# Squared-ReLU layers: running sums of the seven products in PSUM, sums of weight blocks by adding transfers

## The chip, the core and the metric

One Trainium2 chip, one core, one launch. The metric is device time in microseconds, the median of repeated executions of the whole program. The core's engines are named as in the profile: PE (TensorE, matrix products), ACT (ScalarE), DVE (VectorE), POOL (GpSimd) and SP (SyncE, which issues nearly all transfers). SBUF is the on-chip memory, PSUM the small memory in which matmuls add up.

## The reference

Four residual layers on an input of 512 frames by 1024 features in float32: banded attention, a squared-ReLU layer (the MLP), a Griffin recurrent block, a second MLP, each with an RMS norm ahead; at the end one more norm. The change lies in the two MLPs:

```python
def sq_relu_mlp(h, w1, w2):          # w1: 1024 x 4096, w2: 4096 x 1024
    z = jax.nn.relu(jnp.einsum('bsd,df->bsf', h, w1))
    return jnp.einsum('bsf,fd->bsd', z * z, w2)
...
        h = h + sq_relu_mlp(rmsnorm(h, norm_mlp[layer]), mlp_w1[layer], mlp_w2[layer])
```

## The kernel before

**Arithmetic.** A float32 operand is kept as two tiles, H (rounded) and L (what is left over), and each product is three matmuls, H by H, H by L and L by H (`mm3`, lines 202 to 204). So each block of weights, once it has landed, is cast by ACT (`wh`, line 132) and subtracted by DVE (`wl`, line 135) before PE can use it. A weight unit is one such pair of 128 x 1024.

**Weight units.** `plan` is a list of units in the order in which PE uses them. `fetch` issues the transfer, the cast and the subtraction of the next one; `want` hands units to PE, and keeps fetching some units ahead. Eight buffers hold `wh` and `wl` in the MLPs, so the cast of a unit waits until PE has done with the unit eight places ahead of it.

**MLP.** The hidden width of 4096 is cut in eight stretches of 512, the groups g = 0 to 7. Group 0 is computed plainly (tiles `u`). Groups 1 to 7 use a scheme with seven products in place of eight: 512 rows and 256 columns of w1 make a block, and four blocks, 11, 21, 22 and 12, make a group. Beside the blocks themselves the scheme needs four sums of them, s1 = 21 + 22, s3 = 11 + 21, s2 = s1 + 11 and s4 = s2 + 12. Before, DVE makes them in place (lines 128 and 129, tiles `b`). On the other side stand the pieces B11, B21, B22 of the normed input and four sums of them, t1 to t4, made once in a layer. A product is 24 matmuls of 128 x 256 into a PSUM tile `p`. PSUM has two pools that matter here: "at" for the products and "mm" for `d` and `u`, with four buffers each.

The seven products go into four quarters of the group's result (`cA` and `cB`, each 128 x 2 x 512, with a left half LO and a right half HI). Written with P for a product: cA LO = P1 + P2; cA HI = P1 + P6 + P5 + P3; cB HI = P1 + P6 + P7 + P5; cB LO = P1 + P6 + P7 + P4. Before, ACT copies P1 out (line 646, into `w`) and DVE adds the others from PSUM, one by one (lines 651 to 666). Then follow ReLU with the norm's factor (line 628), the square (ACT, line 619), the split into `zH` (ACT, line 622) and `zL` (DVE, line 623).

**Down units.** The second weight matrix multiplies `z` of a group into eight PSUM tiles `d`, each of 12 matmuls of 128 x 512, which DVE adds to the residual `h` (line 678). While the products of group g run, the down units of group g − 1 are placed between them: two after the second product, one after each of the next four, two after the last. So PE runs products and down units in turn, and four weight units of the down kind (`plain`) stand between the seven of a group in `plan`.

**Order.** Each engine runs its own queue in a fixed order. A scheduler sets these orders when the program is built, from the order in the code and its own estimates of when operands are ready; on the chip an instruction whose operand isn't there holds everything behind it on its engine. SP issues the loads of the blocks (line 123); each of the four block tiles `b11`, `b21`, `b22`, `b12` has one buffer, so a group's load waits for the last use of the same tile in the group before.

Names in what follows: `wh43` is the cast unit 43 of the plan; `cA00` and `cB00` are the result of layer 0, group 0; `zH001` its second half; `p201` the product P2 of layer 0, group 1; `d000` and `d001` the first two down tiles; a trailing number after an underscore is a buffer's number.

Of the kernel before, what the change touches and what calls it, by code (L numbers as in the profile page):

```python
# [15 lines left out]
P = 128  # L16
# [24 lines left out]
def trunk(ctx: ExitStack, tc: tile.TileContext, xT, cols, win, wqkv, wo, rwin, rga, rgx, rwo, w1, w2, out):  # L41
# [54 lines left out]
    raws, start_ = {}, []  # L96

    def fetch():
# [20 lines left out]
        else:  # L119
            if kind == "11":  # L120
                for name, src in zip(("11", "21", "22", "12"), srcs):
                    raws[name] = state["raw"].tile([P, 1024], F32, name=f"b{name}_{i}", tag=f"b{name}")
                    nc.sync.dma_start(raws[name].rearrange("p (k c) -> p k c", k=4), src.rearrange("(k p) c -> p k c", p=P))

            for name, at_, with_ in (("s1", "21", "22"), ("s2", "22", "11"), ("s4", "12", "22")):
                if kind == name:
                    if kind == "s1":
                        V.tensor_add(raws["11"], raws["11"], raws["21"])
                    V.tensor_add(raws[at_], raws[at_], raws[with_])
            raw = raws[{"s1": "21", "s2": "22", "s3": "11", "s4": "12"}.get(kind, kind)]  # L130
# [4 lines left out]
        low = V.tensor_sub(L[:, :n], raw[:, :n], f(H[:, :n]))  # L135
        if not i:
            start_.append(low)
# [33 lines left out]
    def add_mlp(layer):  # L171
        starts.append(len(plan))
        for g in range(9):
# [4 lines left out]
            if g < 8:  # L178
                rows, cs = (slice(0, T), slice(T, D)), (slice(g * T, g * T + U), slice(g * T + U, (g + 1) * T))
                srcs = [w1[layer][rows[k], cs[c]] for k, c in ((0, 0), (0, 1), (1, 1), (1, 0))]  # L180
                up_ = [(kind, 4, srcs) for kind in ("11", "s1", "12", "22", "s2", "s4", "s3")]
# [19 lines left out]
    def mm3(acc, WH, WL, XH, XL, start, stop):  # L201
        PE.matmul(acc, WH, XH, start=start, stop=False)  # L202
        PE.matmul(acc, WH, XL, start=False, stop=False)  # L203
        PE.matmul(acc, WL, XH, start=False, stop=stop)  # L204
# [335 lines left out]
    def constants(behind):  # L540

        ap = cst[:, C_AP : C_AP + KT]
        e, ng, zz, z2 = (per.tile([P, KT], F32, name=f"sp{i}") for i in range(4))
# [34 lines left out]
    def mlp(ly, norm, nxt, halves):  # L578
        with ExitStack() as mctx:
# [29 lines left out]
            def product(acc, xs):  # L609
                WH, WL = want(1)  # L610
                for j in range(2):
                    for k, (XH, XL) in enumerate(xs):
                        mm3(acc[:, j * U : (j + 1) * U], WH(k, PAIR[j]), WL(k, PAIR[j]), XH, XL, k == 0, k == 3)
# [19 lines left out]
            def up(g):  # L633
# [7 lines left out]

                cA = cp.tile([P, 2, T], F32, name=f"cA{ly}{g}", tag="cA")
# [3 lines left out]
                S.copy(w, acc["1"])  # L646
                yield
                one("5", t1)
                yield
                one("2", B21)  # L650
                V.tensor_add(cA[:, :, LO], acc["2"], w)
                yield
                one("4", t4)
                yield
                one("6", t2)
                V.tensor_add(w, acc["6"], w)
# [277 lines left out]
```

## Time and profile before

| | |
|---|---|
| median of 3 runs | 1082.8 us (1082.6 to 1083.53) |
| profiled execution | 1082.37 us, span 1080.6 us |
| PE busy | 1069.6 us (99%) |
| DVE busy | 863.5 us (80%) |
| ACT busy | 531.3 us (49%) |
| POOL busy | 9.0 us (1%) |
| transfers | 111.15 MB, mean 103 GB/s |
| mean granted TensorE clock | 0.998 |

The span runs from the first to the last instruction in the trace. Busy time is time in which an engine executes; waiting isn't counted. The table's shares are means over the span; the windows below show them by stage. Layer 0's MLP lies at about 250 to 585 us, layer 1's at about 735 to 1070; the seven-product groups of layer 0 begin at 268.6, those of layer 1 at 751.7.

### The profile page before, as it was taken

What the parts mean: (1) busy time and instruction counts of PE and PEld (TensorE: products, weight loads), DVE (VectorE), ACT (ScalarE), POOL (GpSimd) and SP (SyncE); (2) the same over time, 40 slices, a digit from 0 to 9 for tenths busy, and PEclk for the clock granted to TensorE, in tenths of its full rate; (3) what the DMA queues carried; (4) which work ended last, traced back from release to release, by engine and by line L of the source; (5) the groups of instructions that cost most, each with busy time, mean ns of one, the idle gap of its engine ahead of it and who ended that gap; (6) DMA issues with size and microseconds to landing.
All of it is one profiled execution on the core that took longest, in us unless ns stands there. A gap on an engine that the chain in (4) does not pass through costs nothing.

```text
span 1080.6 us, 15337 instructions
## 1 busy us (share of the span) xinstructions
PE 1069.6 (99%) x6046; PEld 935.6 (87%) x6046; DVE 863.5 (80%) x1286; ACT 531.3 (49%) x775; POOL 9.0 (1%) x28
## 2 busy tenths in 40 slices
PE   9999999999999999999999999999999999999996
PEld 7888888888899999898988888888889999989896
DVE  6889788879887787776777989879887777787665
ACT  6667567565443343342444688366443343343321
POOL 0010000000000000000000000000000000000000
PEclk9999999999999999999999999999999999999999
DMA  8354253341432323322232222442431432332102
GB/s 275 98 140 134 59 176 98 83 152 59 137 117 79 117 89 107 99 81 96 76 122 77 78 64 73 151 142 68 147 117 59 136 98 79 117 94 83 59 1 79
DMA packets 112919, 111.15 MB, mean 103 GB/s; under 512 B 4176, under 2 KB 106704, under 8 KB 112848
## 3 DMA queue, kind: packets, MB, share of 16 engines
q1 hardware_dynamic: 112560, 109.99, 33.1%
q8 instruction: 47, 0.77, 0.3%
q14 instruction: 24, 0.20, 0.1%
q10 hardware_dynamic: 288, 0.20, 0.1%
HBM read 103.87 MB, written 2.10 MB: 98 GB/s over the span
## 4 chain that ended last, share of the span: by engine, by line
PE 96%; DVE 2%; ACT 1%; DMA 1%; issue 0%; SPq 0%; DVEq 0%; ACTq 0%
PE d L203 11%; PE d L202 11%; PE d L204 11%; PE p L204 9%; PE p L203 9%; PE p L202 9%; PE x L414 1%; PE wo L203 1%; PE wo L202 1%; PE ro L202 1%; PE v L202 1%; PE ro L204 1%; PE v L204 1%; PE wo L204 1%; PE xb L202 1%; PE xb L204 1%
## 5 line engine op out<-in xcount | busy, mean ns | idle before, releaser
L132 ACT CAST wh<-wr 128x1024 fp32r<-128x1024 f32 (+1 forms) x129 | 133.6, 1039 | 201.6 <-PE d L203 88.8
L203 PE MATMUL d<-zL,wh 128*128 128x512 f32 (+1 forms) x544 | 206.3, 379 | 0.0
L202 PE MATMUL d<-zH,wh 128*128 128x512 f32 (+1 forms) x544 | 205.1, 379 | 0.0
L204 PE MATMUL d<-zH,wl 128*128 128x512 f32 (+1 forms) x544 | 204.8, 377 | 0.0
L132 ACT CAST wh<-b 128x1024 fp32r<-128x1024 f32 x98 | 101.3, 1047 | 174.8 <-PE p L203 76.0
L135 DVE TENSOR_TENSOR wl<-wr,wh 128x1024 fp32r<-128x1024 f32 (+1 forms) x130 | 156.2, 1203 | 23.3 <-ACT wh L132 23.1
L135 DVE TENSOR_TENSOR wl<-b,wh 128x1024 fp32r<-128x1024 f32 x98 | 118.7, 1219 | 42.9 <-ACT wh L132 42.8
L204 PE MATMUL p<-tH,wl 128*128 128x256 f32 x448 | 126.8, 283 | 0.0
L203 PE MATMUL p<-tL,wh 128*128 128x256 f32 x448 | 126.8, 283 | 0.0
L202 PE MATMUL p<-tH,wh 128*128 128x256 f32 x448 | 126.6, 282 | 0.0
L204 PEld LDWEIGHTS d<-zH,wl 128*128 128x128 f32 x544 | 102.4, 188 | 19.1
L202 PEld LDWEIGHTS d<-zH,wh 128*128 128x128 f32 x544 | 102.5, 189 | 16.8
L203 PEld LDWEIGHTS d<-zL,wh 128*128 128x128 f32 x544 | 102.7, 189 | 16.3 <-DVE zL L623 0.5
L678 DVE TENSOR_TENSOR h<-d,h 128x512 f32<-128x512 f32 x120 | 82.2, 686 | 38.9 <-PE d L204 38.3
L204 PE MATMUL p<-hnH,wl 128*128 128x256 f32 x336 | 95.1, 283 | 0.0
L203 PE MATMUL p<-hnL,wh 128*128 128x256 f32 x336 | 95.1, 283 | 0.0
L202 PE MATMUL p<-hnH,wh 128*128 128x256 f32 x336 | 94.9, 282 | 0.0
L202 PEld LDWEIGHTS p<-tH,wh 128*128 128x128 f32 x448 | 85.8, 192 | 1.6
L203 PEld LDWEIGHTS p<-tL,wh 128*128 128x128 f32 x448 | 85.8, 192 | 1.6
L204 PEld LDWEIGHTS p<-tH,wl 128*128 128x128 f32 x448 | 85.8, 192 | 0.0
L202 PEld LDWEIGHTS p<-hnH,wh 128*128 128x128 f32 x336 | 64.3, 191 | 1.7
L203 PEld LDWEIGHTS p<-hnL,wh 128*128 128x128 f32 x336 | 64.3, 191 | 1.6
(336 smaller groups left out, 2071.6 us busy)
## 6 DMA issues: line engine op xcount, KB each, us to landing
wr<-in_w SPq DMA_DIRECT2D x72, 512.0 KB, 3.5
b<-in_w SPq DMA_DIRECT2D x56, 512.0 KB, 4.4
wr<-in_wqkv SPq DMA_DIRECT2D x20, 512.0 KB, 4.0
wr<-in_rwin SPq DMA_DIRECT2D x16, 512.0 KB, 3.6
wr<-in_wo SPq DMA_DIRECT2D x8, 512.0 KB, 4.2
wr<-in_rwo SPq DMA_DIRECT2D x8, 512.0 KB, 3.4
x<-in_xT SPq DMA_DIRECT2D x8, 256.0 KB, 4.3
bias<-in_win SPq DMA_DIRECT2D x4, 512.0 KB, 4.5
```

The lines of the kernel that those rows point to most:

```text
L132: S.copy(H[:, :n], raw[:, :n])
L135: low = V.tensor_sub(L[:, :n], raw[:, :n], f(H[:, :n]))
L202: PE.matmul(acc, WH, XH, start=start, stop=False)
L203: PE.matmul(acc, WH, XL, start=False, stop=False)
L204: PE.matmul(acc, WL, XH, start=False, stop=stop)
L414: PE.transpose(b[:, c : c + P], pt[:, seg[t] + kt * P : seg[t] + (kt + 1) * P], ident)
L678: V.tensor_add(hT[m], acc, hT[m])
```

## The change

**Sums of weight blocks.** The four additions of DVE in a group go. In their place POOL issues four transfers a group that read a block from DRAM and add it onto a tile in SBUF (`accum_op=ALU.add`). Block 22 is added onto tile 21 right behind the loads: s1. Block 21 is added onto tile 11, once 11 itself has been cast and subtracted: s3. Block 11 is added onto tile 21, once s1 has been cast and subtracted: s2. Block 12 is added onto tile 21, once s2 has been: s4. The order of the units in `plan` and of the loads changes accordingly.

**Running sums in PSUM.** A group uses three product tiles in place of seven. P6, P7 and P4 run on in the tile of P1, and P3 runs on in that of P5. Between them ACT copies the intermediate sums out: P1 to cA LO, P1 + P6 to cA HI, the last sum to cB LO, and P5 to `w`. DVE adds three times from PSUM in place of seven. The next product on a tile waits for the copy or addition that reads it. The order of the products becomes P1, P5, P2, P6, P7, P3, P4.

**Small things.** The small tiles of `constants` lie in a work tile, and the scratch memory for transfers that POOL issues is doubled.

```diff
@@ -93,7 +93,7 @@
 
     plan = []
     state = {"next": 0, "ready": [], "ahead": 4, "stop": None, "more": None, "units": 0}
-    raws, start_ = {}, []
+    raws, srcs_, start_ = {}, {}, []
 
     def fetch():
         i = state["next"]
@@ -117,22 +117,25 @@
                 queue.dma_start(rv[:, :, c0 : c0 + w], src.rearrange("(k p) c -> p k c", p=P))
                 c0 += w
         else:
+
+            def view(name):
+                return raws[name].rearrange("p (k c) -> p k c", k=4)
+
             if kind == "11":
-                for name, src in zip(("11", "21", "22", "12"), srcs):
+                srcs_.update(zip(("11", "21", "22", "12"), (src.rearrange("(k p) c -> p k c", p=P) for src in srcs)))
+                for name in ("11", "21", "12", "22"):
                     raws[name] = state["raw"].tile([P, 1024], F32, name=f"b{name}_{i}", tag=f"b{name}")
-                    nc.sync.dma_start(raws[name].rearrange("p (k c) -> p k c", k=4), src.rearrange("(k p) c -> p k c", p=P))
-
-            for name, at_, with_ in (("s1", "21", "22"), ("s2", "22", "11"), ("s4", "12", "22")):
-                if kind == name:
-                    if kind == "s1":
-                        V.tensor_add(raws["11"], raws["11"], raws["21"])
-                    V.tensor_add(raws[at_], raws[at_], raws[with_])
-            raw = raws[{"s1": "21", "s2": "22", "s3": "11", "s4": "12"}.get(kind, kind)]
+                    nc.sync.dma_start(view(name), srcs_[name])
+                G.dma_start(view("21"), srcs_["22"], accum_op=ALU.add)
+            raw = raws[{"s1": "21", "s2": "21", "s3": "11", "s4": "21"}.get(kind, kind)]
         if i:
             S.copy(H[:, :n], raw[:, :n])
         else:
             start_.append(V.tensor_copy(H[:, :n], raw[:, :n]))
         low = V.tensor_sub(L[:, :n], raw[:, :n], f(H[:, :n]))
+        for done, name, src in (("11", "11", "21"), ("s1", "21", "11"), ("s2", "21", "12")):
+            if kind == done:
+                G.dma_start(view(name), srcs_[src], accum_op=ALU.add)
         if not i:
             start_.append(low)
         state["ready"].append((nk, H[:, :n].rearrange("p (k c) -> p k c", k=nk), L[:, :n].rearrange("p (k c) -> p k c", k=nk)))
@@ -178,7 +181,7 @@
             if g < 8:
                 rows, cs = (slice(0, T), slice(T, D)), (slice(g * T, g * T + U), slice(g * T + U, (g + 1) * T))
                 srcs = [w1[layer][rows[k], cs[c]] for k, c in ((0, 0), (0, 1), (1, 1), (1, 0))]
-                up_ = [(kind, 4, srcs) for kind in ("11", "s1", "12", "22", "s2", "s4", "s3")]
+                up_ = [(kind, 4, srcs) for kind in ("11", "s1", "12", "s2", "s3", "s4", "22")]
             else:
                 up_ = []
             dn = [("plain", 4, [w2[layer][(g - 1) * T : g * T, u * U : (u + 1) * U]]) for u in range(4)]
@@ -198,10 +201,10 @@
     add_mlp(1)
     state["stop"] = starts[0] + 4
 
-    def mm3(acc, WH, WL, XH, XL, start, stop):
-        PE.matmul(acc, WH, XH, start=start, stop=False)
-        PE.matmul(acc, WH, XL, start=False, stop=False)
-        PE.matmul(acc, WL, XH, start=False, stop=stop)
+    def mm3(acc, WH, WL, XH, XL, start, stop, shared=False):
+        PE.matmul(acc, WH, XH, start=start, stop=False, skip_group_check=shared)
+        PE.matmul(acc, WH, XL, start=False, stop=False, skip_group_check=shared)
+        PE.matmul(acc, WL, XH, start=False, stop=stop, skip_group_check=shared)
 
     def project(accs, cols_, WH, WL, xs, mid=None):
 
@@ -540,7 +543,8 @@
     def constants(behind):
 
         ap = cst[:, C_AP : C_AP + KT]
-        e, ng, zz, z2 = (per.tile([P, KT], F32, name=f"sp{i}") for i in range(4))
+        room = wk.tile([P, T], F32, name="room", tag="nsq", bufs=2)
+        e, ng, zz, z2 = (room[:, i * KT : (i + 1) * KT] for i in range(4))
         after(V.tensor_scalar(ng, ap, -1.0, None, ALU.mult), behind)
         V.tensor_tensor(e, ap, ng, ALU.max)
         S.activation(e, e, AF.Exp, scale=-1.0)
@@ -606,11 +610,14 @@
             sum_ = lambda n: [(tH[k][:, n], tL[k][:, n]) for k in range(4)]
             B11, B21, B22 = own(0, LO), own(4, LO), own(4, HI)
 
-            def product(acc, xs):
+
+
+            def product(acc, xs, fresh=True):
                 WH, WL = want(1)
                 for j in range(2):
                     for k, (XH, XL) in enumerate(xs):
-                        mm3(acc[:, j * U : (j + 1) * U], WH(k, PAIR[j]), WL(k, PAIR[j]), XH, XL, k == 0, k == 3)
+                        c = acc[:, j * U : (j + 1) * U]
+                        mm3(c, WH(k, PAIR[j]), WL(k, PAIR[j]), XH, XL, fresh and j == 0 and k == 0, k == 3, True)
 
             def pair(acc):
                 return acc.rearrange("p (j c) -> p j c", j=2)
@@ -639,31 +646,33 @@
                     product(acc[n], xs)
                     acc[n] = pair(acc[n])
 
+                def more(n, xs):
+                    product(acc[n].rearrange("p j c -> p (j c)"), xs, False)
+
                 cA = cp.tile([P, 2, T], F32, name=f"cA{ly}{g}", tag="cA")
                 cB = cp.tile([P, 2, T], F32, name=f"cB{ly}{g}", tag="cB")
                 w = pair(wk.tile([P, T], F32, name=f"w{ly}{g}", tag="nsq", bufs=2))
                 one("1", B11)
-                S.copy(w, acc["1"])
+                S.copy(cA[:, :, LO], acc["1"])
                 yield
                 one("5", t1)
+                S.copy(w, acc["5"])
                 yield
                 one("2", B21)
-                V.tensor_add(cA[:, :, LO], acc["2"], w)
+                V.tensor_add(cA[:, :, LO], acc["2"], cA[:, :, LO])
                 yield
-                one("4", t4)
+                more("1", t2)
+                S.copy(cA[:, :, HI], acc["1"])
                 yield
-                one("6", t2)
-                V.tensor_add(w, acc["6"], w)
-                V.tensor_add(cA[:, :, HI], acc["5"], w)
+                more("1", t3)
+                V.tensor_add(cB[:, :, HI], acc["1"], w)
                 yield
-                one("3", B22)
-                V.tensor_add(cA[:, :, HI], acc["3"], cA[:, :, HI])
+                more("5", B22)
+                V.tensor_add(cA[:, :, HI], acc["5"], cA[:, :, HI])
                 relu2(g, 0, cA, ALU.max)
                 yield
-                one("7", t3)
-                V.tensor_add(w, acc["7"], w)
-                V.tensor_add(cB[:, :, LO], acc["4"], w)
-                V.tensor_add(cB[:, :, HI], acc["5"], w)
+                more("1", t4)
+                S.copy(cB[:, :, LO], acc["1"])
                 relu2(g, 1, cB, ALU.min)
                 yield
 
@@ -920,7 +929,7 @@
         "rwin": a["rec_w_in"][0], "rga": a["rec_w_ga"][0], "rgx": a["rec_w_gx"][0], "rwo": a["rec_w_o"][0],
         "w1": a["mlp_w1"], "w2": a["mlp_w2"],
     }
-    nc = _bacc.Bacc("TRN2", target_bir_lowering=False, num_devices=1, dynamic_dma_scratch_size=1024)
+    nc = _bacc.Bacc("TRN2", target_bir_lowering=False, num_devices=1, dynamic_dma_scratch_size=2048)
     arrays, args = {}, []
     for name, v in arrs.items():
         v = np.ascontiguousarray(v)
```

What this does to the engines' queues at the places that matter, as the two programs stand (not how long anything takes). First ACT in the first group of layer 0's MLP, before:

```order
L132 CAST wh41_2682<-b12_38_2666 128x1024
L132 CAST wh42_2741<-wr42_2743 128x1024
L646 COPY w01_2817<-p101_2818 128x512
L619 ACTIVATE cA00_2656<-cA00_2656 128x1024
L622 CAST zH000_2780<-cA00_2656 128x1024
L619 ACTIVATE cB00_2657<-cB00_2657 128x1024
L132 CAST wh44_2819<-b22_38_2664 128x1024
L622 CAST zH001_2811<-cB00_2657 128x1024
L132 CAST wh45_2850<-wr45_2852 128x1024
```

and after:

```order
L132 CAST wh43_2748<-b21_38_2662 128x1024
L132 CAST wh44_2821<-b11_38_2660 128x1024
L132 CAST wh45_2851<-wr45_2853 128x1024
L132 CAST wh41_2683<-b12_38_2664 128x1024
L132 CAST wh42_2742<-wr42_2744 128x1024
L626 ACTIVATE cA00_2656<-cA00_2656 128x1024
L629 CAST zH000_2782<-cA00_2656 128x1024
L132 CAST wh46_2882<-b21_38_2662 128x1024
L626 ACTIVATE cB00_2657<-cB00_2657 128x1024
L656 COPY cA01_2817<-p101_2820 128x2x256
L629 CAST zH001_2813<-cB00_2657 128x1024
L659 COPY w01_2819<-p501_2850 128x512
```

The casts of s2 (`wh43`), s3 (`wh44`) and the next down unit (`wh45`) moved ahead of the two casts that stood first; s4 (`wh46`) stands between the split of `cA00` and the square of `cB00`. Both `wh43` and `wh46` read tile 21, and so an adding transfer.

PE in the same group, behind P5 (the second product in its order), before:

```order
L202 MATMUL d000_2885<-zH000_2780,wh40_2676 128x512
L202 MATMUL d001_2899<-zH000_2780,wh40_2676 128x512
L202 MATMUL p201_2913<-hnH4_80,wh41_2682 128x256
L203 MATMUL p201_2913<-hnL4_88,wh41_2682 128x256
L204 MATMUL p201_2913<-hnH4_80,wl41_2683 128x256
L202 MATMUL p201_2913<-hnH5_81,wh41_2682 128x256
L203 MATMUL p201_2913<-hnL5_89,wh41_2682 128x256
L203 MATMUL d000_2885<-zL000_2781,wh40_2676 128x512
```

and after (the fourth row shown is the first to use `zH001`, the eighth the first to use `zL001`; three rows that read like the first three are left out):

```order
L205 MATMUL d000_2886<-zH000_2782,wh40_2677 128x512
L206 MATMUL d000_2886<-zL000_2783,wh40_2677 128x512
L207 MATMUL d000_2886<-zH000_2782,wl40_2678 128x512
...
L205 MATMUL d000_2886<-zH001_2813,wh40_2677 128x512
L205 MATMUL d001_2900<-zH000_2782,wh40_2677 128x512
L206 MATMUL d001_2900<-zL000_2783,wh40_2677 128x512
L207 MATMUL d001_2900<-zH000_2782,wl40_2678 128x512
L206 MATMUL d000_2886<-zL001_2814,wh40_2677 128x512
L207 MATMUL d000_2886<-zH001_2813,wl40_2678 128x512
```

Before, matmuls of `p201` are mixed into the two down tiles; after, the 24 matmuls of `d000` and `d001` stand together and `p201` follows them.

POOL issues four transfers in each group, such as the first four here: s1, s3, s2, s4 (the fifth begins the next group).

```order
L129 DMA b21_82_4108<-in_w1 128x4x256
L138 DMA b11_82_4106<-in_w1 128x4x256
L138 DMA b21_82_4108<-in_w1 128x4x256
L138 DMA b21_82_4108<-in_w1 128x4x256
L129 DMA b21_93_4477<-in_w1 128x4x256
```

ACT in the same stretch, after, where unit 83 is s1:

```order
L132 CAST wh83_4157<-b21_82_4108 128x1024
L665 COPY cA04_3957<-p104_3960 128x2x256
L132 CAST wh84_4187<-wr84_4189 128x1024
L132 CAST wh85_4207<-b12_82_4110 128x1024
L132 CAST wh86_4256<-wr86_4258 128x1024
```

Before, POOL had no instruction in the MLPs, and no copy from PSUM stood between these casts.

## The prediction

> **What bounds the kernel now.** I read the engines and the chain of waits on the page first, then the busy time by stretch, the costliest groups, the DMA issues, and last the timelines where a layer begins.
>
> ```profile
> PE 1069.6 (99%) x6046; PEld 935.6 (87%) x6046; DVE 863.5 (80%) x1286; ACT 531.3 (49%) x775; POOL 9.0 (1%) x28
> ...
> PE 96%; DVE 2%; ACT 1%; DMA 1%; issue 0%; SPq 0%; DVEq 0%; ACTq 0%
> ```
>
> ```profile
> 0.00:130.00 130.00, 128.25 (x647) 107.92 (x648) 107.24 (x251) 88.15 (x191) 7.16 (x23) 1.00 0.52 147
> 130.00:250.00 120.00, 118.98 (x593) 99.16 (x592) 100.98 (x214) 75.04 (x154) 1.87 (x5) 1.00 0.39 119
> 250.00:1000.00 750.00, 749.88 (x4317) 661.49 (x4316) 603.82 (x738) 345.01 (x397) 0.00 (x0) 1.00 0.32 99
> 1000.00:1080.60 80.60, 72.46 (x495) 67.05 (x493) 51.45 (x85) 23.12 (x35) 0.00 (x0) 0.97 0.14 46
> ```
>
> The second fence has one stretch a row: its length, then the busy time of PE, PEld, DVE, ACT and POOL. TensorE (PE) is the bound and it isn't a mean that hides a stage: in the 750 us that hold both MLPs but the end of the second, it stands for 0.12 us. All it lacks in the whole span is 1.75 + 1.02 + 0.12 + 8.14 = 11.0 us, 1% of it, and most of that lies in the final norm, which the change doesn't touch. So the change can't gain by relieving VectorE (DVE) or ScalarE (ACT) as such. What matters is whether it makes PE stand.
>
> **What is removed from the vector engines.**
>
> ```profile
> L129 DVE TENSOR_TENSOR b<-b,b 128x1024 f32<-128x1024 f32 x42 | 51.1, 1216 | 0.0
> L128 DVE TENSOR_TENSOR b<-b,b 128x1024 f32<-128x1024 f32 x14 | 17.1, 1224 | 0.4
> L660 DVE TENSOR_TENSOR cA<-p,cA 128x512 f32<-128x512 f32 x14 | 9.7, 691 | 27.0 <-PE p L204 27.0
> L646 ACT COPY w<-p 128x512 f32<-128x512 f32 x14 | 8.2, 586 | 2.1 <-PE p L204 2.1
> L132 ACT CAST wh<-b 128x1024 fp32r<-128x1024 f32 x98 | 101.3, 1047 | 174.8 <-PE p L203 76.0 <-DVE b L129 50.9 <-DMA b<-in_w 20.4
> L135 DVE TENSOR_TENSOR wl<-b,wh 128x1024 fp32r<-128x1024 f32 x98 | 118.7, 1219 | 42.9 <-ACT wh L132 42.8
> ```
>
> There are 14 groups (7 in each layer). Each loses four block additions (51.1 + 17.1 = 68.2 us over the run) and four of its seven PSUM additions (56 x 0.69 = 38.6 us), so DVE falls from 863.5 to about 757 us. ACT gains three copies a group: 42 x 0.59 = 24.6 us, to about 556. Neither is on the path: both have slack under PE, and the 50.9 us that ACT waited for L129 were hidden, as the 0.12 us show. These edits cost and gain nothing; PE's back-to-back matmuls cover them. The matmul count is unchanged (24 per product, 12 per down unit), and a running sum in PSUM is the same instruction with another start flag. The small tiles of `constants` and the larger scratch size add no instruction on a path: nothing.
>
> The new waits of PE are for ACT's copies: the product t3 must wait until the sum after t2 has been copied out (0.59 us). A down unit lies between them (12 matmuls), so 2.7 us are there for it. That too is nothing, unless ACT is held by something ahead of the copy. This leads to the transfers.
>
> **The price of one adding transfer.** No row of before shows POOL issuing a DMA, or a DMA that adds. The nearest rows:
>
> ```profile
> wr<-in_w SPq DMA_DIRECT2D x72, 512.0 KB, 3.5
> b<-in_w SPq DMA_DIRECT2D x56, 512.0 KB, 4.4
> ...
> graw<-in_rga SPq DMA_DIRECT2D x4, 128.0 KB, 2.6
> ```
>
> The plain load of these blocks takes 4.4 us from issue to landing (four are issued together), 3.5 us where less stands around it. An adding transfer also reads 512 KB of its destination. From the 128 KB and 512 KB rows, 384 KB more cost 0.9 us, so another 512 KB costs at least 1.2 us; POOL's own issuing is unseen. Lower bound 3.5 (the second reading fully hidden), upper 13.2 (three passes, read, read and write, of 4.4 each). I take L = 6.3 us, an estimate: 4.4, 1.2 for the second reading, 0.7 for POOL. It stays near the lower end since the nearest row is the same block from the same tensor. The Trainium skill, "DMA: Bandwidth & Descriptors", section "Anatomy of one DMA — SWDGE (gpsimd) path", gives about 2.0 us plus bytes over 436e3 for a transfer that POOL issues, an estimate of 3.2 us here. It says nothing on one that adds; by it the sum below would be 0, and no row here shows a transfer of POOL's. The 56 transfers move 28 MB more beside 110, with the queues a third busy: bandwidth isn't the limit.
>
> **The steady group.** Block 21 now goes through a chain: load, +22, cast and subtract (s1), +11, cast and subtract (s2), +12, cast and subtract (s4), and only then the next load into the only buffer.
>
> ```profile
> 395.14 0.28 PE L202 MATMUL p<-hnH,wh 128*128 128x256 f32 x1
> ...
> 437.18 0.28 PE L202 MATMUL p<-hnH,wh 128*128 128x256 f32 x1
> ```
> ```profile
> 414.93 1.05 ACT L132 CAST wh<-b 128x1024 fp32r<-128x1024 f32 x1 [4.57 <-PE p L203]
> ```
>
> One group takes 437.18 − 395.14 = 42.0 us of PE. Casts run eight weight units ahead, each let go when PE has ended with an older unit (the bracket: ACT waited 4.57 us for PE). The cast of the next s1 comes 414.93 − 395.14 = 19.8 us into the group. The cast of s4 is freed by the group's first product, at 2.9 us (24 matmuls, some 0.12 us apart); with its 1.05 and the subtraction's 1.22 block 21 is free at 5.2. Load 4.4: 9.6. So the first adding transfer has 19.8 − 9.6 = 10.2 us before ACT stands, and I put the limit at about 9.7 for small delays between. The window of s2 (cast at about 33.7) is 33.7 − 19.8 − 2.3 = 11.6. With L = 6.3 the twelve later groups cost 0.
>
> **The first group of each MLP.** Here the order that is written into the engines' queues matters. In the timelines (start, length, operation; ACT, DVE, PE):
>
> ```profile
> 265.88 1.06 ACT L132 CAST wh<-b 128x1024 fp32r<-128x1024 f32 x1 [3.02 <-PE u L203]
> ...
> 272.24 1.07 ACT L619 ACTIVATE cA<-cA 128x1024 f32<-128x1024 f32 x1
> 273.33 1.05 ACT L622 CAST zH<-cA 128x1024 fp32r<-128x1024 f32 x1
> 274.29 1.05 ACT L619 ACTIVATE cB<-cB 128x1024 f32<-128x1024 f32 x1
> 275.25 1.03 ACT L132 CAST wh<-b 128x1024 fp32r<-128x1024 f32 x1
> 276.18 1.05 ACT L622 CAST zH<-cB 128x1024 fp32r<-128x1024 f32 x1
> ```
> ```profile
> 262.11 1.22 DVE L135 TENSOR_TENSOR wl<-b,wh 128x1024 fp32r<-128x1024 f32 x1
> ...
> 264.99 3.34 DVE L256 RECIPROCAL nm1r<-nm1r 128x512 f32<-128x512 f32 x1
> ...
> 274.42 1.23 DVE L623 TENSOR_TENSOR zL<-cA,zH 128x1024 fp32r<-128x1024 f32 x1 [0.36 <-ACT zH L622]
> ...
> 277.83 1.22 DVE L623 TENSOR_TENSOR zL<-cB,zH 128x1024 fp32r<-128x1024 f32 x1
> ```
> ```profile
> 274.44 0.73 PE L202 MATMUL d<-zH,wh 128*128 128x512 f32 x2
> 275.01 0.28 PE L202 MATMUL p<-hnH,wh 128*128 128x256 f32 x1
> ...
> 275.70 0.50 PE L203 MATMUL d<-zL,wh 128*128 128x512 f32 x1
> ```
>
> Before, the first down matmuls (274.44) could start ahead of zL, because PE's order put five matmuls of the second product between them (275.01), and again further on ahead of the second half, zL of cB, which ends at 277.83 + 1.22 = 279.05. The changed order does two things. PE now has all 24 matmuls of these two down units in a row, with the second product behind them. They need zH of cB about 6 matmuls after 274.4 (6 x 0.23 = 1.4: 275.8) and zL of cB four later (276.7). On ACT, the cast of s4 (`wh46`) now stands ahead of the square of cB, and the cast of s2 (`wh43`) ahead of both squares. Each waits for an adding transfer, so the square of cB waits too.
>
> The chain, step by step. Without two of the additions the subtraction of s1 (before: 262.11 to 263.33) ends at about 259.5, 2 x 1.2 us and some casts earlier, and the reciprocal runs from 263.2 to 266.5. The +11 transfer lands at 259.6 + 6.3 = 265.9; cast 1.05: 266.95; subtraction, now that the reciprocal is over, 1.2: 268.15. The +12 transfer, issued 0.1 later, lands at 274.55. Then ACT does wh46, the square of cB, one copy from PSUM and the cast of cB, at the pitch of the rows above (274.29 − 273.33 = 0.96; copies 0.5): 274.55 + 0.97 + 0.97 + 0.5 + 1.05 = 278.05, and zL ends 1.25 later at 279.3. PE wanted it at 276.7: it stands 2.6 us, where before it stood some 0.2 in small gaps.
>
> The same sum from L, for this layer: 0.4 us at L = 4, 1.2 at 5, 2.7 at 6.3, 4.2 at 7, 6.2 at 8. Each us of L counts twice once the subtraction no longer hides behind the reciprocal (259.6 + L + 1.05 above 266.5, L above 5.85).
>
> ```profile
> 745.37 3.34 DVE L256 RECIPROCAL nm2r<-nm2r 128x512 f32<-128x512 f32 x1
> ...
> 759.26 0.50 PE L203 MATMUL d<-zL,wh 128*128 128x512 f32 x1
> ```
>
> The second MLP's head has the same order on both engines, with its reciprocal before at 745.37 and PE's last gap of before in front of 759.26. The same arithmetic from there gives 0.15, 0.7, 2.6, 4.0 and 5.9 us for these five L.
>
> **Sum.** 0 (DVE, ACT) + 0 (PSUM) + 0 (steady groups) + 2.7 + 2.6 − 0.3 (gaps of before that go under) = +5.0 us. The profiled execution took 1082.37 us (span 1080.6 and 1.8 around it), 0.4 below the median of 1082.8; so 1087.4 for it, and 1087.8 against the median. Times within 0.2% (2.2 us) can't be told from no change here.
>
> **Rivals.**
> - *The transfers are quick (L up to about 5.2).* The two heads then cost up to 2.3 us together and the time stays at 1083 to 1085. For it: 3.5 us in the `wr` row, and little else moves at the heads. The rule of the Trainium skill above (3.2 us) would give this too. Against: a second operand must be read, and POOL must write out 512 rows of 1 KB. Chance 0.28.
> - *Block 21 becomes the bound (L above 9.7).* What is missing in s1's window makes ACT late, and the load of the next group with it; above the limit each us of L costs some 2 us a group, 24 over twelve groups, beside heads of about 19. L = 10.2 gives 19 + 12 = +31 us, L = 11 about +55. For it: three passes of 4.4 are 13.2. Against: it needs half as much again as my estimate. The Trainium skill, "SBUF — State Buffer", section "Who interferes with whom", has a way there: POOL can't write its transfer's descriptors while DVE runs in a two-port mode. It excepts two-input adds; DVE's rows beside these windows are such (1.22 us per 1024 elements), and no run yet shows a lockout. Chance 0.12.
> - *Faster.* DVE has 106 us less to do. In the end stretch (8.1 us without matmuls) the last group's evictions lead to the last down units and the final norm; if DVE and not PE times that end, 2 x 1.22 + 4 x 0.69 = 5.2 us less of it could pull the end forward by up to that, with 0.3 from the gaps at the heads: 1077.3 to 1080.5. It decides if L is below 4 as well, so that the heads give nothing back. Against: the windows show PE busy up to 1000 us, and after the last products only down units follow, which don't use what was removed. Chance 0.06.
>
> **How the numbers follow.** The forecast, slower through the two heads, covers L from 5.2 to 9.7: +2.3 to +12 up to L = 8, then to +19. It has 0.54, and its centre is +5.0: 1087.8. Quick transfers hold 0.28 and end as no change. The bound by block 21 (0.12) and the forecast make 0.66 slower; faster is 0.06. The range goes from 1082 (quick transfers, nothing lost) to 1102 (heads at L = 9.7, +19): it leaves out the faster case and most of the bound by block 21, under 2 in 10. The forecast's own range is 1085 to 1102.
>
> **What would show it.** In the changed profile: DVE near 757 us, ACT near 556; POOL's transfers landing after 5.2 to 8 us; ACT waiting for such a transfer just ahead of the square of cB, and PE standing 2 to 3 us for zL or zH of cB, some 5 us behind the start of its second product, in each MLP's head; no gap in the twelve later groups. PE gaps that come back every 42 us mean block 21 bounds; no gap at the heads means L under 5 or another order of events. The prediction is wrong in kind if PE loses time at the PSUM waits of t3, where I counted none.

## The result, and the profile after

The changed kernel takes 1090.89 us (median of 6 runs, 1087.95 to 1092.05) against 1082.74 before (median of 6 runs too): a ratio of 1.0067, 95% interval 1.0057 to 1.0077. It is slower by 8.2 us. Forecast were 1087.8 us, between 1082 and 1102, and slower with a chance of 0.66. The execution with the profile took 1090.57 us with a span of 1088.8.

The page of the changed kernel, engines and chain:

```profile
PE 1074.2 (99%) x6046; PEld 938.7 (86%) x6046; DVE 772.3 (71%) x1174; ACT 550.6 (51%) x817; POOL 81.8 (8%) x84
...
PE 92%; DMA 2%; DVE 2%; ACT 2%; issue 0%; DVEq 0%; POOL 0%; ACTq 0%; POOLq 0%
```

DVE has lost 91 us, ACT gained 19, POOL 73. PE has the same 6046 matmuls, yet is busy 4.6 us longer: some of them ran slower, as is seen below. In windows of the changed kernel (length, busy time of PE, PEld, DVE, ACT, POOL, then the granted clock, share and rate of the DMA engines), first the stretch that stood 0.12 us before, then the later groups of both layers alone:

```profile
250.00:1000.00 750.00, 745.89 (x4267) 656.51 (x4266) 513.06 (x628) 358.95 (x432) 68.75 (x53) 1.00 0.57 136
```
```profile
300.00:550.00 250.00, 250.00 (x1574) 227.04 (x1573) 154.36 (x186) 104.35 (x115) 28.53 (x22) 1.00 0.61 142
800.00:1000.00 200.00, 200.00 (x1262) 181.74 (x1262) 119.02 (x123) 81.47 (x89) 24.64 (x19) 1.00 0.66 154
```

In the later groups PE never stands, with the DMA engines twice as busy as before (a share of 0.61 and 0.66, against 0.31 and 0.32). Nearly all that is lost lies in the two first groups: the time from P1 of group 1 to P1 of group 2 was 42.44 us in layer 0 and 42.18 in layer 1; now it is 46.37 and 46.20. That is +3.93 and +4.02, together 7.95 of the 8.2 us in the spans. The head of layer 0 after the change, ACT, then DVE, then PE:

```profile
265.51 2.00 ACT L132 CAST wh<-b 128x1024 fp32r<-128x1024 f32 x2 [3.93 <-DMA b<-in_w]
...
271.89 1.06 ACT L626 ACTIVATE cA<-cA 128x1024 f32<-128x1024 f32 x1 [1.54 <-DVE cA L711]
...
274.77 1.05 ACT L132 CAST wh<-b 128x1024 fp32r<-128x1024 f32 x1 [0.73 <-DMA b<-in_w]
275.72 1.05 ACT L626 ACTIVATE cB<-cB 128x1024 f32<-128x1024 f32 x1
276.68 0.56 ACT L656 COPY cA<-p 128x512 f32<-128x512 f32 x1
277.15 1.05 ACT L629 CAST zH<-cB 128x1024 fp32r<-128x1024 f32 x1
```
```profile
269.44 1.23 DVE L135 TENSOR_TENSOR wl<-b,wh 128x1024 fp32r<-128x1024 f32 x1 [1.62 <-ACT wh L132]
270.58 1.28 DVE L711 SCALAR_TENSOR_TENSOR cA<-u,nm1r 128x512 f32<-128x512 f32 x2
...
278.23 1.23 DVE L630 TENSOR_TENSOR zL<-cB,zH 128x1024 fp32r<-128x1024 f32 x1 [0.63 <-ACT zH L629]
```
```profile
274.27 0.39 PE L205 MATMUL d<-zH,wh 128*128 128x512 f32 x1
275.38 0.50 PE L206 MATMUL d<-zL,wh 128*128 128x512 f32 x1 [0.71 <-DVE zL L630]
...
276.42 0.39 PE L207 MATMUL d<-zH,wl 128*128 128x512 f32 x1
278.24 1.13 PE L205 MATMUL d<-zH,wh 128*128 128x512 f32 x2 [1.44 <-ACT zH L629]
279.17 0.63 PE L206 MATMUL d<-zL,wh 128*128 128x512 f32 x1
279.60 0.63 PE L207 MATMUL d<-zH,wl 128*128 128x512 f32 x1
```

ACT waits for an adding transfer (in brackets, `DMA b<-in_w`) at the casts of s2 and of s4; behind the second stand the square of cB, one copy and the cast of cB. The first wait (3.93 us) acts by way of DVE: it holds up the casts behind it, DVE stands for one of them, and cA, which comes next in DVE's order, is late with it. PE stands at 275.38 for the first zL and at 278.24 for the half of cB. From 278.4 on a matmul of 128x512 starts every 0.427 us (279.17 to 279.60), not every 0.229. The windows of this place, cut where the clock changes:

```profile
274.95:278.37 3.42, 1.55 (x6) 0.99 (x7) 2.79 (x4) 3.42 (x5) 0.00 (x0) 1.00 0.72 201
278.37:281.78 3.41, 3.41 (x9) 2.63 (x10) 3.35 (x3) 1.26 (x2) 0.00 (x0) 0.50 0.80 264
281.78:285.19 3.41, 3.41 (x21) 2.97 (x20) 1.45 (x3) 1.05 (x1) 0.00 (x0) 1.00 0.85 253
```

For 3.41 us the granted clock is 0.50. The same stands in layer 1 from 766.47 to 769.88.

### The profile page after: what moved, and what is told of

It reads as the page before. It is cut to its first block, busy times and chain, and to the rows that moved or that the text cites. A ratio compares the mean times of both kernels' runs of the same rounds, so it can differ in the third digit from the quotient of the medians.

```text
span 1088.8 us, 15387 instructions
## 1 busy us (share of the span) xinstructions
PE 1074.2 (99%) x6046; PEld 938.7 (86%) x6046; DVE 772.3 (71%) x1174; ACT 550.6 (51%) x817; POOL 81.8 (8%) x84
## 4 chain that ended last, share of the span: by engine, by line
PE 92%; DMA 2%; DVE 2%; ACT 2%; issue 0%; DVEq 0%; POOL 0%; ACTq 0%; POOLq 0%
PE d L205 11%; PE d L206 11%; PE d L207 10%; PE p L207 8%; PE p L206 8%; PE p L205 8%; DMA b<-in_w 2%; PE x L417 1%; PE wo L205 1%; PE wo L206 1%; PE ro L205 1%; PE v L205 1%; PE v L207 1%; PE ro L207 1%; PE wo L207 1%; PE v L206 1%
## 5 line engine op out<-in xcount | busy, mean ns | idle before, releaser
L207 PEld LDWEIGHTS d<-zH,wl 128*128 128x128 f32 x544 | 103.4, 190 | 19.7
L138 POOL DMA_DIRECT2D b<-in_w x42 | 54.6, 1299 | 345.1 <-DVE wl L135 243.3
```

Source lines behind the costliest of these rows:

```text
L138: G.dma_start(view(name), srcs_[src], accum_op=ALU.add)
L207: PE.matmul(acc, WL, XH, start=False, stop=stop, skip_group_check=shared)
```

## The experiments

The theory (A in most of them): the cast of s4 holds cB back on ACT, PE's new order has no other work there, PE stands, and its clock falls because it stood. The rivals put the loss on the running sums in PSUM, or on the transfers' traffic as such.

**ACT's order.** One order is added for the first group of each layer: the unit with `i - 12 in starts` is its s4, and `state["split"]` is at that point the last cast of cB.

```diff
-            S.copy(H[:, :n], raw[:, :n])
+            cast = S.copy(H[:, :n], raw[:, :n])
+            if i - 12 in starts:
+                after(cast, state["split"])
...
-                S.copy(zH, c)
+                state["split"] = S.copy(zH, c)
```

> The changed kernel, with one order added: in the first group of each MLP, ACT's cast of s4 (wh46 and its like in the second layer) stands behind the cast of cB (zH001) and not ahead of its square. All transfers and running sums stay. Theory A (ACT's queue stood behind an adding transfer, cB came late, PE stood and its clock then fell): zH001 ends near 276.3 us and zL001 near 277.5, so PE stands about 0.9 us for the first zL and 0.6 for the second in each head, no row of the clock falls below 0.9, time near 1085 us. Rival B (the time is lost to the running sums or to the transfers' traffic, wherever the cast stands): stays within 1.5 us of 1090.5.

It took 1085.82 us, 1.0025 of before (1.0015 to 1.0035): 5.1 of the 8.2 us are gone. PE stands about 1.5 us in the worst 3.41 us of layer 0's head, 1.0 in layer 1's, and the clock holds:

```profile
275.18:278.59 3.41, 2.32 (x9) 1.63 (x10) 3.41 (x4) 3.38 (x6) 0.00 (x0) 1.00 0.68 203
278.59:282.00 3.41, 3.41 (x17) 2.80 (x16) 3.28 (x4) 0.99 (x2) 0.00 (x0) 1.00 0.81 251
```

Theory A holds, rival B fails. Of the 3.0 us that remain, 2.7 lie in the two heads, where PE stands for both zL (in layer 0 about 0.8 us for each). The wait at s2 is untouched (3.87 us), so cA is as late as in the changed kernel.

**The running sums alone.** The sums of blocks are made by DVE again, all else is as in the changed kernel.

```diff
-                G.dma_start(view("21"), srcs_["22"], accum_op=ALU.add)
+            if kind == "s1":
+                V.tensor_add(raws["11"], raws["11"], raws["21"])
+                V.tensor_add(raws["21"], raws["21"], raws["22"])
+            if kind == "s2":
+                V.tensor_add(raws["21"], raws["11"], raws["22"])
+            if kind == "s4":
+                V.tensor_add(raws["21"], raws["21"], raws["12"])
...
-        for done, name, src in (("11", "11", "21"), ("s1", "21", "11"), ("s2", "21", "12")):
-            if kind == done:
-                G.dma_start(view(name), srcs_[src], accum_op=ALU.add)
```

> The running sums, the unit order and the product order of the changed kernel; the four sums of blocks are made by DVE from four loaded blocks, no transfer of POOL's. Theory A: heads of the MLPs lose nothing and the groups keep their 42.0 us; 1082.7 us, at most 0.5 either way. Rival B (the copies and waits of the running sums cost PE something): some tenths of a us in each of the 14 groups, 1086 to 1090.

1083.48 us, 1.0004 (0.9995 to 1.0013): no difference. The running sums and their new waits cost nothing, nor do the small things, which this kernel has too, as the prediction had it. They gain nothing either, though DVE has less to do.

**The adding transfers alone.** The fetch of the changed kernel in the kernel before, with the small things of the change.

```diff
-            for name, at_, with_ in (("s1", "21", "22"), ("s2", "22", "11"), ("s4", "12", "22")):
...
+                G.dma_start(view("21"), srcs_["22"], accum_op=ALU.add)
...
+        for done, name, src in (("11", "11", "21"), ("s1", "21", "11"), ("s2", "21", "12")):
+            if kind == done:
+                G.dma_start(view(name), srcs_[src], accum_op=ALU.add)
```

> The adding transfers alone: the kernel before with its unit order, its seven product tiles and DVE evictions, where the four sums are made by POOL's transfers as in the changed kernel. In the first groups only the cast of s2 (wh44) stands ahead of the squares, s4 behind zH001. Theory A: cA's split comes about 2 us late, PE stands some 2.5 us at each head and its clock falls after it; +3 to +4.5 us a head, 1088 to 1091. Rival B (only the running sums cost): 1083.

1092.77 us, 1.0094 (1.0078 to 1.0110), a little above the upper end of what was expected. The whole loss comes with the transfers, without a running sum. The clock fell in both heads (0.50 for 3.41 us from 278.44 and from 766.55). Here ACT's order puts the square of cB ahead of the cast of cA, and PE stands for cA's zL (ACT, DVE, PE):

```profile
262.16 1.05 ACT L132 CAST wh<-b 128x1024 fp32r<-128x1024 f32 x1 [2.30 <-DMA b<-in_w]
```
```profile
263.77 0.69 DVE L605 SCALAR_TENSOR_TENSOR tL<-ht,tH 128x512 fp32r<-128x512 f32 x1 [2.30 <-ACT tH L604]
```
```profile
275.22 0.73 PE L205 MATMUL d<-zH,wh 128*128 128x512 f32 x2
277.72 0.50 PE L206 MATMUL d<-zL,wh 128*128 128x512 f32 x1 [1.77 <-DVE zL L627]
```

ACT's wait for a transfer holds a cast that DVE needs, so DVE stands as long, 2.30 us, and from 263.77 to the zL of cA it has no gap. So the instruction that is late differs from order to order; that something in the head waits for a transfer doesn't.

**PE kept busy.** Two kernels put matmuls whose result nobody reads where PE stood. The first puts 7 in one place:

```diff
-                project([acc], [PAIR[m % 2]], WH, WL, [z[g, k] for k in range(4)])
+                fill = None
+                if (g, m) == (0, 0):
...
+                    def fill():
+                        for _ in range(7):
+                            PE.matmul(spare_, WH(0, PAIR[0]), z[0, 0][0], start=True, stop=True, skip_group_check=True)
...
+                project([acc], [PAIR[m % 2]], WH, WL, [z[g, k] for k in range(4)], fill)
```

> The changed kernel with 7 matmuls of 128x512 whose result nobody reads, put on PE where it stood 1.8 us for zH001, in each MLP's first group. Data come as late as before. Theory A (the clock falls because PE stands, and the fall costs some 1.5 us a head beside the standing): granted clock stays above 0.95 behind the filler, mean 0.997 or more, time about 1087.5, smaller spread of the runs. Rival B (the clock falls for another reason, such as the transfers' traffic): clock 0.993 as in the changed kernel and 1090.5 us.

1090.71 us, 1.0063 (1.0051 to 1.0076): not the 1087.5 expected. In layer 0 the filler was too short; in the profiled execution cB came late enough that PE still stood 2.3 us of one stretch of 3.41, and the clock fell at 281.24. In layer 1 it stood 1.1 us in its worst stretch and the clock held. The other four runs had a mean clock of 0.997 or 0.998, yet two of them took 1090.71 and 1090.8 us; they have no trace, so what they lost is open. The second kernel fills all three places (4, 7 and 3 matmuls on operands that are there early):

```diff
+                            for _ in range({(0, 1): 4, (2, 0): 7, (2, 1): 3}.get((k, n), 0)):
+                                last = PE.matmul(fill, WH(0, c), hnH[0], start=True, stop=True, skip_group_check=True)
...
+                            if (k, n) in ((0, 1), (2, 0), (2, 1)):
+                                after(ins, last)
```

> The changed kernel with unread matmuls of 128x512 in all three places where PE stood in a head: 4 ahead of the first zL, 7 ahead of the first zH001, 3 ahead of the first zL001; three matmuls of d001 that stood between these come behind. Theory A (the half clock follows a stretch of 3.41 us in which PE stood over some 1.5 to 2.0 us, as the traces so far have it): no half clock in the heads, mean clock 0.997, the heads lose what the late data cost (2.7 us) and some 0.7 for the three matmuls, 1088.5 us. Rival B: half clock again in the heads, 1091.

The clock held in both heads:

```profile
275.49:278.90 3.41, 2.94 (x13) 2.08 (x12) 2.13 (x2) 3.32 (x4) 0.00 (x0) 1.00 0.73 214
278.90:282.32 3.42, 3.20 (x13) 2.34 (x14) 3.28 (x3) 1.54 (x3) 0.00 (x0) 1.00 0.74 230
```

With the transfers, their traffic and the late data all in place, a busy PE keeps its clock; the mean clock of all five runs was 0.996 to 0.998, the same as before the change. So the clock fell because PE stood. The time is 1090.95 us all the same (1.0073, 1.0061 to 1.0086), not 1088.5. In the profiled execution the head of layer 1 is 0.9 us shorter than in the changed kernel (45.30), that of layer 0 is 0.25 longer (46.62): its cast of s4 began at 275.58, not 274.77, for the transfer came later, and three useful matmuls stand behind the filler. An estimate from the traces accounts for both heads: the clock gave back 1.4 us in layer 0 and 1.6 in layer 1, the three matmuls behind the filler took 3 x 0.23 = 0.7 in each, and the later transfer 0.8 in layer 0, which makes +0.1 and −0.9. This execution, at 1089.41 us, was the fastest of the five; the others have no trace. Filler isn't a remedy here; the test is one of the cause.

**PE's order.** P2 of the first group goes ahead of the first two down units, its weight unit with it; ACT's order stays as changed.

```diff
-                plan.extend(up_[0:2] + dn[0:1] + up_[2:3] + dn[1:2]
+                head = dn[0:1] + up_[2:3] if g > 1 else up_[2:3] + dn[0:1]
+                plan.extend(up_[0:2] + head + dn[1:2]
...
-                    for _ in range((0, 2, 1, 1, 1, 1, 2)[n]):
+                    for _ in range(((0, 2, 1, 1, 1, 1, 2) if g > 1 else (0, 0, 3, 1, 1, 1, 2))[n]):
```

> The changed kernel with P2 of the first group of each MLP placed ahead of the first two down units on PE (its weight unit moves with it); ACT's order keeps the cast of s4 ahead of the square of cB. Theory A (the head loses time because PE's new order has nothing left between P5 and the down units to cover a late cB): the 24 matmuls of P2 (2.9 us) cover it; zH001 at 278.2 is needed at 278.5, zL001 at 279.5 at 278.8, so PE stands about 0.7 us a head, the clock holds, 1083.5 us. Rival B (the late cast of s4 on ACT costs the same wherever PE's order puts P2): 1089 to 1091.

1083.69 us, 1.0007 (0.9998 to 1.0015). Covered by P2, the late cB costs next to nothing, and rival B falls. Either order is enough to take most of the loss away: the loss needs both a late cB and a PE with nothing else to do.

**The heads by DVE.** The first group's sums are made by DVE as in the second experiment (`first` marks its units), the other twelve groups keep the transfers.

```diff
+                if i - 4 in starts:
+                    pass
+                else:
...
+            first = any(start + 4 <= i < start + 15 for start in starts)
+            if first and kind == "s1":
...
-            if kind == done:
+            if kind == done and not first:
```

> The changed kernel, where the four sums of the first group of each MLP are made by DVE; the twelve later groups keep the adding transfers, all groups the running sums. Theory A (the later groups cost nothing, all of the loss lies in the two heads): 1082.8 us, within 0.7 either way. Rival B (the transfers' traffic costs something all along): 1085 or more, in proportion to 12 of 14 groups.

1084.03 us, 1.0011 (1.0002 to 1.0020), 1.2 above what was expected and below the 1085 of the rival. In the profiled execution 0.4 us are lost in the second group of layer 0, the first with transfers, almost none in those behind; the rest isn't placed. 48 of the 56 transfers cost about 1 us together (up to 2 by the interval).

**What adding costs.** POOL's transfers overwrite and don't add.

```diff
-                G.dma_start(view("21"), srcs_["22"], accum_op=ALU.add)
+                G.dma_start(view("21"), srcs_["22"])
...
-                G.dma_start(view(name), srcs_[src], accum_op=ALU.add)
+                G.dma_start(view(name), srcs_[src])
```

> The changed kernel, where POOL's 56 transfers overwrite their tile and don't add (the sums are left out). It prices the adding: by the prediction's split (4.4 as a load, 1.2 for reading the destination, 0.7 for POOL) issue to landing falls from 6.0 to about 4.8 us and, with the prediction's table, the heads cost 0.7 to 1.2 us each, no fall of the clock, 1084.5 us. Rival B (the length is POOL's issuing and the queue, adding costs nothing): 6.0 and 1090.5. Rival C (POOL's transfers cost 3.2 us when they don't add): heads cost nothing, 1083.

1082.82 us, 0.9999 (0.9990 to 1.0007). DMA issues and the group of POOL's issuing instructions, first of the changed kernel, then of this one:

```profile
b<-in_w SPq DMA_DIRECT2D x56, 512.0 KB, 4.8
b<-in_w POOLq DMA_DIRECT2D x56, 512.0 KB, 6.0
...
L138 POOL DMA_DIRECT2D b<-in_w x42 | 54.6, 1299 | 345.1 <-DVE wl L135 243.3 <-DMA b<-in_w 34.9 <-issue 25.0
```
```profile
b<-in_w POOLq DMA_DIRECT2D x56, 512.0 KB, 4.1
...
L138 POOL DMA_DIRECT2D b<-in_w x42 | 31.6, 752 | 362.7 <-DVE wl L135 342.3 <-ACT nm2r L258 10.2 <-ACT nm1r L258 10.2
```

Adding costs 1.9 us from issue to landing (6.0 against 4.1): 0.55 of it is POOL's own instruction (1.30 against 0.75 us), the rest, 1.35, lies behind it. At 4.1 the heads take 42.45 and 42.15 us from P1 to P1, as before the change (42.44 and 42.18). ACT, in layer 0:

```profile
263.95 2.00 ACT L132 CAST wh<-b 128x1024 fp32r<-128x1024 f32 x2 [1.99 <-DMA b<-in_w]
...
270.33 1.06 ACT L626 ACTIVATE cA<-cA 128x1024 f32<-128x1024 f32 x1 [0.41 <-DVE cA L711]
```

The wait at s2 is 1.94 us shorter than in the changed kernel (1.99 against 3.93), and the square of cA, counted from the start of P1, is 1.94 us earlier; at s4 ACT doesn't wait at all. So both waits, and PE's standing for the first zL with the first of them, go back to the length of a transfer. Rival C had the effect right and its 3.2 us wrong.

**Both orders.** ACT's order of the first experiment and PE's of the swap together, transfers and running sums kept.

> The changed kernel with both orders of the first group set: P2 ahead of the first two down units on PE, and ACT's cast of s4 behind the cast of cB. All transfers and running sums stay. Theory A (late cB and missing cover are the whole loss): zH001 near 276.5 us, zL001 near 278, both ahead of PE, no gap over 0.4 us in the heads, no half clock; 1082.9 us, at most 0.5 either way. Rival B (the adding transfers cost something beyond the heads): 1084 or more.

1082.32 us, 0.9997 (0.9988 to 1.0006): the loss is gone. The stretch with both MLPs and its casts of the first head:

```profile
250.00:1000.00 750.00, 749.87 (x4319) 662.09 (x4318) 519.02 (x636) 364.54 (x438) 70.16 (x55) 1.00 0.57 137
```
```profile
274.43 1.06 ACT L629 ACTIVATE cB<-cB 128x1024 f32<-128x1024 f32 x1 [0.19 <-DVE cB L716]
275.52 1.05 ACT L632 CAST zH<-cB 128x1024 fp32r<-128x1024 f32 x1
```

PE lacks 0.13 us in 750, as before (0.12). This is the version that keeps the change at no cost. It isn't faster than the kernel before, since PE was full there too.

**The limit in the later groups.** In groups 2 to 7 the transfer ahead of s1 is made twice.

```diff
-                G.dma_start(view("21"), srcs_["22"], accum_op=ALU.add)
+                for _ in range(1 if i - 4 in starts else 2):
+                    G.dma_start(view("21"), srcs_["22"], accum_op=ALU.add)
```

> The changed kernel, where in groups 2 to 7 of each MLP the first adding transfer (+22, ahead of s1) is made twice, the second behind the first; so s1 to s4 come out with block 22 added twice. It asks for the limit that the prediction put at 9.7 us: issue to landing becomes about 12.0 for s1 alone. Theory A (the prediction's rule, 2 us a group for each us above 9.7): 2.3 x 2 x 12 = 55 us more, 1146. Theory B (the windows of s2 and s4, with 11.6 and more against 6.0, take the delay up, so that a group loses only what s1's cast is late for the copy behind it, 1.0 to 1.3 us): 1103 to 1107, the standing ahead of P7 (the product on t3), no half clock there. Theory C (ACT's order has slack enough): 1091.

1139.57 us, 1.0528 (1.0511 to 1.0545): 48.7 us above the changed kernel. That is near theory A's 55, but by luck: from the first issue to the second landing the doubled transfers took 12.2 to 16.6 us, not 12.0, and with these lengths A's rule gives some 89 us (twice what each of the twelve has above 9.7, added up). The loss is spread otherwise than A has it, too. From the start of P1 in one group to the next, layer 0's groups 2 to 6 take 44.1, 56.0, 44.2, 44.3 and 43.1 us in place of 42.05. So groups 2 and 4 to 6 lose 1.1 to 2.2 us each, where theory B has 1.0 to 1.3, and group 3 loses 14. There ACT waited 12.1 us for the transfer ahead of s1, and PE 6.3 us for the copy behind that cast: the delay of group 2 had come through to the next load, whose adding transfer was issued 19.7 us after P1, in place of 10.8. The clock fell in that group too (from 371.77 and from 392.25 on), which theory B had excluded. The waits of PE in this run (total, times, longest):

```profile
PE p L206 <- ACT cA L666: 21.8, 8, 6.4
PE d L206 <- ACT zH L630: 12.8, 6, 2.9
```

Neither theory is right as a whole. That a limit lies between 8 and 12 us is shown (in the changed kernel the longest transfer ahead of s1 in a later group took 7.9 us, and nothing was lost; the shortest doubled one took 12.2), and that above it PE stands for the copy of the running sum (L666) behind the cast of s1. The 9.7 us themselves weren't tested.

## Why the prediction was right, and where it was off

- *Nothing from DVE and ACT, nothing from the running sums, nothing in the later groups.* Right: the running sums alone change nothing (1.0004), and PE has no gap from 300 to 550 and from 800 to 1000 us. DVE fell by 91 us, not 106, and ACT rose by 19, not 25. The instructions are as counted: the lengths of DVE's rows, added up, fell by 104 us (933.0 to 828.6), those of ACT's rose by 24.5. But where rows follow closely, one's length runs into the next one's (before: 262.11 + 1.22 against 263.25), and busy time counts that once.
- *The price of an adding transfer, 6.3 us.* 6.0 was measured. The parts were off in ways that cancel: 4.4 for the load where a plain one of POOL's takes 4.1 with 0.75 of issuing in it, 0.7 for POOL where the adding form takes 1.30, 1.2 for the second reading where 1.35 were measured. In layer 0's head the two transfers that the chain needs took 5.9 and 6.5 us. The 56 transfers moved 29.4 MB, not 28. For its rival the prediction set against this the Trainium skill's "DMA: Bandwidth & Descriptors", section "Anatomy of one DMA — SWDGE (gpsimd) path", with an estimate of 3.2 us. Neither the plain transfer (4.1) nor the adding one agrees with it.
- *The head of layer 0, step by step.* +12 was to land at 274.55; the cast of s4 began at 274.77. zH of cB was to end at 278.05: 278.20. zL at 279.3: 279.46. PE's standing was put at 2.7 and 2.6 us; added up from starts of matmuls that come later than 0.229 us after the one before, it was 2.86 and 2.54. The prediction put all of it on the second half and overlooked the standing for the first zL (0.9 us of it in layer 0), which comes from the wait at s2 by way of DVE. The total came out because the last operand sets it: zL of cB ended at 279.46, and PE, with 10 matmuls of 0.229 us from 274.27 on, would have wanted it at 276.6.
- *The table from L.* For L = 4 it had 0.4 and 0.15 us of standing; the transfers that only overwrite (4.1) have 0.4 and 0.1. But by the rows of before, which the prediction shows, ACT is busy with cA's split until 274.4, so a quicker transfer alone couldn't let s4's cast begin much sooner, and the prediction doesn't say why the standing should fall with L. It fell because cA came earlier too: with the transfers that overwrite its split ended at 272.5.
- *The term that was missing: the clock.* The sum +5.0 knew only of standing. Behind it PE ran 3.41 us at half clock, 7 matmuls in layer 0 at 0.427 us in place of 0.229: 1.4 us; 1.6 in layer 1. These 3.0 us are nearly all of the difference between +5.0 and +8.2. So the mechanism of the standing and its size were right, the sum was 3 us short, and 1090.89 lies in the range because that was left wide for longer transfers. The trace of before shows the half clock only at the program's end, where nothing waits for PE.
- *The bound by block 21.* Not reached at 6.0. For the doubled transfer the rule of 2 us per us and group gives 89 us with the measured lengths; 48.7 were lost, and unevenly.
- *POOL held up by DVE*, the second way into that rival: POOL's issuing instruction took 1.29 to 1.31 us in all 42 on line 138; 41 of them ran beside DVE's two-input instructions, one beside none (1.29). So these don't hold POOL up. The Trainium skill, "SBUF — State Buffer", section "Who interferes with whom", excepts two-input adds, and that agrees. DVE ran nothing else beside them, so whether its other modes would hold POOL up wasn't tried.

## What to carry to other kernels

When a sum moves from an engine to a transfer, look at the first use after a stage begins: there the chain has no lead, and whatever stands behind the waiting cast in the engine's fixed order waits with it, and by way of that cast also what stands behind its user on another engine. Compare both queues there, the one that waits and the one that is waited for; either a short reorder of the first or a product moved ahead on the second took the loss away. And a relief of an engine that isn't the bound, here 91 us of DVE, is worth nothing by itself.

## What the runs showed of the hardware

The clock of PE falls on a fixed grid. In each of these traces all half-clock stretches begin a whole number of 3.413 us apart (278.37 and 766.47 in the changed kernel: 143.0 steps) and last one step, or more where PE stood on. Counting, for each step at full clock, how long PE stood in it (a start more than 0.26 us after the one before, less 0.23): in the traces of all twelve kernels here, up to the last norm, the clock fell after every step with 2.04 us or more (2.04, 2.07, 2.13, 2.25, 2.27, 2.30, 2.48, 2.95, 3.18 and so on) and after none with 1.73 or less (1.73, 1.60, 1.47, 1.17 and below). One of the latter, in the kernel with the doubled transfer:

```profile
1037.37:1040.78 3.41, 1.84 (x11) 1.34 (x10) 1.29 (x2) 2.37 (x3) 1.28 (x1) 1.00 0.11 14
1040.78:1044.20 3.42, 3.42 (x26) 3.20 (x25) 2.43 (x4) 1.16 (x2) 0.00 (x0) 1.00 1.10 175
```

At the program's end, in the last norm, this count fails: there the clock fell in every trace, after steps with 0.6 to 1.5 us of standing. The matmuls there are small, many of them with 2 columns, and the count takes each start for a whole matmul. If each matmul is given a time by its columns (0.229 us for 512), all steps behind which the clock fell have 2.04 us or more without work, and the largest behind which it held has 1.98 (before, from 1068.9 on; the step in which PE starts is left out). So the bound lies near 2.0 of 3.41 us in these traces.

The grid doesn't begin with the program: its first step begins 0.24 to 3.13 us behind the first instruction, differently in each trace, so the same head lies elsewhere on it. That fits the spread of the changed kernel's six runs, where the two with a mean clock of 0.996 and 0.997 took 1088.57 and 1087.95 us and the four with 0.993 to 0.995 took 1090.57 to 1092.05; only one of these has a trace, so it isn't shown. If it is so, the two runs without a fall lie close to the prediction's 1087.8, which had none. The Trainium skill, "TensorE: Matmul & The Clock Gate", section "Part 1: The HAM clock gate (the "warmup" mystery)", has this window (3413 ns, free-running) and the half clock, and both agree. Its condition differs: it lets the clock fall after an idle window, and here it fell also after windows in which PE had worked for up to 40% of the time.
